# Five of eleven pairs of SwiGLU tiles as seven products of quarters, with weight sums prepared on GpSimd during the input stage

## The chip, the cores and the metric

One core of a Trainium2 chip runs the kernel. The metric is device time in microseconds (us), from one launch of the whole program. Before the change it took 819.53 us, the median of 3 runs (818.77 to 819.92). A measurement is a device time; the profile is one further execution with the hardware profiler on.

## The reference, cut to what matters

One hybrid decoder block in float32, on 512 tokens (T) of width 1024 (D), batch 1, depth 1; the SwiGLU width is 2816.

```python
h = rmsnorm(x, norm1_g)
z = h @ w_in + b_in                              # 1024 -> 6656 columns
z_glu, z_rx, z_rg, z_ga, z_gb = split(z)
u = z_glu[..., :1024] * sigmoid(z_glu[..., 1024:])
y_a = silu(layernorm(causal_conv31(u))) @ conv_w_out + conv_b_out
xb = causal_conv4(z_rx)
y_b = (rg_lru(xb) * gelu(z_rg)) @ lru_w_out
x = x + (sigmoid(z_ga) * y_a + sigmoid(z_gb) * y_b) @ w_mix_out
h = rmsnorm(x, norm2_g)
x = x + (silu(h @ ffn_w1) * (h @ ffn_w3)) @ ffn_w2
return rmsnorm(x, norm_f_g)
```

The change concerns `silu(h @ ffn_w1) * (h @ ffn_w3)` alone; both weights are 1024 x 2816.

## The kernel before

**Numbers.** Each float32 operand is held as two tiles, h (the value cast to the matmul's float32r) and l (the value minus h). A product is three matmuls, h.h, h.l and l.h, which add up in one PSUM bank (`mm3`, L354 to L364; L363 is the matmul). Tokens move: the stationary operand is a 128 x 128 block of weights, the moving one 128 channels by 512 tokens. So a tile of 128 output columns from 1024 inputs is 8 blocks of 3, 24 matmuls of 512 columns.

**Stages.** In order: norm 1; the input stage, which makes all tiles of z in the order that the list `ORDER` gives (62 entries: u, rx, rg, gb, ga are tiles of z, g the small block-diagonal gates of the recurrence, r its scans), with the convolutions on VectorE beside it; lru_w_out (yb), conv_w_out (ya), w_mix_out (mx), norm 2; the SwiGLU stage; the output stage with ffn_w2 (o); and the last norm.

**Weights.** `wchunk` lists all weight chunks in the order of use, and `weights(key)` (L150) hands one out and first emits the list up to four further chunks (AHEAD). `emit_chunk` (L124) takes a raw tile, 128 x 1024 float32, from a pool of 4; loads it by a DMA that the sync engine (SP) issues (L133; L177 for the gates); casts it on ScalarE (ACT, L108) into the h half of one of 5 hl tiles; and subtracts (L104) into the l half. The engine of the subtraction is the argument `lo`: GpSimd (POOL) for w_in and the gates, VectorE (DVE) for all later weights. SP is one queue in program order for all DMAs. A raw tile that has not come free holds SP, and all that is queued behind it. A gate chunk (L168) is put together from small loads. Gates also need rows of neighbouring tiles: `ext_in` (L611 to L623) moves them with small DMAs out of the split tiles of xb, and `gates(j)` (L628 to L643) multiplies them in.

**Seven products, already there.** Two of the matrix products (w_mix_out and ffn_w2) already run by Winograd's form of Strassen's scheme: with both operands cut into quarters, seven products of quarters replace eight. `Quartered` holds the quarters of the weights. Four of the seven weight operands are sums of quarters: t1 = b12 - b11, t2 = b22 - b12 + b11, t3 = b22 - b12, t4 = b21 - t2. `make_sums(k)` makes them for one block row: it loads two raw tiles, runs four 512-column operations on DVE, and stores four results in DRAM (for ffn_w2; 256 KB each), from where they are loaded like weights. `Sevenfold` (from L727) holds the activations' side: `tile` collects the tiles, `pair(k, ua, va)` makes the sums of activations when both tiles of a pair are there, `run` issues the products.

**SwiGLU stage.** The 22 tiles of 128 columns go in pairs k = 0 to 10, tile k and then tile k + 11. A tile is two `mm3` of 512 columns (w1 and w3, banks f1 and f3), then `ffn_out`: a Silu on ACT, and on DVE two products of 256 columns into u or v (L878). With a pair's second tile come `pair` and `outq.make_sums` for ffn_w2. Pair 0 is issued by token halves, 256 columns at a time, because the second half's normalized tokens come later (`turned`, in `turn_half`). Pairs 1 to 10 follow at 512 columns.

**What sets the order.** The program is written for the tile framework, which schedules each engine's instructions by their order of emission and dependences, picks the slots of pools, and adds the semaphores. `issue_after(turned)` keeps what is inside it behind that instruction.

Of the kernel before, what the change touches and what calls it, by code (L numbers as in the profile page):

```python
# [8 lines left out]
F32 = mybir.dt.float32  # L9
F32R = mybir.dt.float32r  # L10
AF = mybir.ActivationFunctionType
ALU = mybir.AluOpType

P = 128
T = 512
# [11 lines left out]
ND = D // P  # L27
NR = DR // P
NF = DF // P
# [8 lines left out]
FEW, MANY = 32, 112  # L38

LAG = 12  # L40


ROWS = [
# [32 lines left out]
def tile_block(ctx, tc, a, out):  # L76
    nc = tc.nc
    pool = lambda name, bufs, **k: ctx.enter_context(tc.tile_pool(name=name, bufs=bufs, **k))
    consts = pool("consts", 1)
    raws = pool("raws", RAW)  # L80
# [4 lines left out]
    def tiles(tag, bufs):  # L85
        p_ = pool(tag, bufs)
        return lambda name, dtype=F32: p_.tile([P, T], dtype, tag=tag, name=name)

    longt, shortt = tiles("long", SLOTS), tiles("short", SHORT)

    def pairt(name, dtype=F32R):

        return longt(f"{name}h", dtype), longt(f"{name}l", dtype)

    def bank(name):
        return psum.tile([P, T], F32, tag="mm", name=name)

    def bank2(name):
        return psum2.tile([P, T], F32, tag="cv", name=name)

    vec, act, pe, pool_e = nc.vector, nc.scalar, nc.tensor, nc.gpsimd

    def sub(eng, o, x, y):
        eng.tensor_tensor(out=o, in0=x, in1=y, op=ALU.subtract)  # L104

    def split_to(h, l, full, eng, copy=act.copy):

        copy(h, full)  # L108
        sub(eng, l, full, h.bitcast(F32))
        return h, l  # L110

    def split(name, full, eng, p_=None, copy=act.copy):
        p_ = p_ or pairt(name)
        return split_to(*p_, full, eng, copy)
# [6 lines left out]
    def wchunk(key, src, kt, cols, where="hl", lo=pool_e, after=None):  # L121
        chunks.append((key, src, kt, cols, where, lo, after))
# [23 lines left out]
    def emit_to(n):  # L146
        while emitted[0] < min(len(chunks), n):
            emit_chunk()

    def weights(key, ahead=AHEAD):  # L150
        i = next(i for i, c in enumerate(chunks) if c[0] == key)
        emit_to(i + 1 + ahead)
        return held.pop(key)
# [36 lines left out]
    ORDER = """u0 u1 rx0 rx1 gb0 rx2 u2 g0 rx3 gb1 g1 u3 rx4 g2 gb2 r0 r1 u4 g3 rx5 rg0 g4 rx6 rg1 u5 r2 r3 g5 rx7  # L190
        gb3 rg2 rx8 g6 rg3 u6 r4 r5 g7 rx9 gb4 rg4 u7 g8 r6 r7 rg5 gb5 g9 rg6 gb6 r8 r9 rg7 gb7 ga0 rg8 ga1 rg9
        ga2 ga3 ga4 ga5 ga6 ga7""".split()
    ORDER = [(t.rstrip("0123456789"), int(t.lstrip("abcdefghijklmnopqrstuvwxyz"))) for t in ORDER]
# [18 lines left out]
    dram = ctx.enter_context(tc.tile_pool(name="dram", bufs=1, space=bass.MemoryType.DRAM))  # L212
# [67 lines left out]
    mixq = Quartered("mx", a["w_mix_out"][0].rearrange("(k p) n -> p k n", p=P), ND // 2, vec, ("t1", "t4"))  # L280
    w1 = a["ffn_w1"][0].rearrange("(k p) n -> p k n", p=P)
    w3 = a["ffn_w3"][0].rearrange("(k p) n -> p k n", p=P)
    ff_order = [j for k in range(NF // 2) for j in (k, k + NF // 2)]
    for j in ff_order:
        wchunk(f"f1_{j}", w1[:, :, j * P : (j + 1) * P], ND, P, lo=vec)
        wchunk(f"f3_{j}", w3[:, :, j * P : (j + 1) * P], ND, P, lo=vec)
    outq = Quartered("o", a["ffn_w2"][0].rearrange("(k p) n -> p k n", p=P), NF // 2, vec)
    x2_kept = [[dram.tile([P, T], F32, tag=f"x2k{t}{h}", name=f"x2k{t}{h}") for h in range(2)] for t in range(NT)]

# [6 lines left out]
    at, col, parts = 0, {}, []  # L296
    for name, n in ROWS:
# [4 lines left out]
        while done < n:  # L302
            m = min(n - done, P - row_at(at + done)[1])
# [50 lines left out]
    def mm3(ps, ws, xs, lo_last=False):  # L354


        n = 3 * len(ws)
        i = 0
        three = [((wh, xh), (wh, xl), (wl, xh)) for (wh, wl), (xh, xl) in zip(ws, xs)]
        if lo_last:  # L360
            three = [q[:2] for q in three] + [q[2:] for q in three]
        for l, r in (q for qs in three for q in qs):
            pe.matmul(ps, l, r, start=i == 0, stop=i == n - 1)  # L363
            i += 1  # L364

    def w_tiles(key, kt, ahead=AHEAD):
        h, l = weights(key, ahead)
        return [(h[:, k, :], l[:, k, :]) for k in range(kt)]
# [41 lines left out]
    def parts_of(pair_tiles, cs=slice(0, T)):  # L410
        return [(h[:, cs], l[:, cs]) for h, l in pair_tiles]
# [9 lines left out]
    HALVES = [slice(0, 256), slice(256, 512)]  # L421
    EARLY = 2
# [42 lines left out]
    ab, e, s, s2, po, c4 = (sm[:, i, :] for i in range(6))  # L465
# [44 lines left out]
    def beside():  # L510
# [18 lines left out]
        def column_mean(name, tot, scale):  # L529

            ps = bank2(f"{name}p")
            for i, v in enumerate(tot):
                pe.matmul(ps, onesr, v, start=i == 0, stop=i == 1)
            act.activation(ps, ps, AF.Copy, scale=scale)
            return ps

        def pause(n):
            for _ in range(n):
                yield
# [6 lines left out]
        tot = split("lnms", tot, vec)  # L546
        yield from pause(LAG)
        mean = column_mean("lnm", tot, 1.0 / DC)
# [10 lines left out]
        tot = split("lnvs", tot, vec)  # L559
        yield from pause(LAG)  # L560
        rs = column_mean("lnv", tot, 1.0 / DC)
# [12 lines left out]
    def run_beside(n):  # L574
        for _ in range(n):
            next(side, None)
# [49 lines left out]
    hs = xb  # L626
# [54 lines left out]
        vec.tensor_tensor(out=ps, in0=hs[j], in1=ps, op=ALU.mult)  # L681
        y.append(split(f"y{j}", ps, vec))

    for kind, j in ORDER:
        if kind == "u":
            glu(j)
        elif kind == "rx":
            rx(j)
            run_beside(4)
        elif kind == "g":  # L690
            gates(j)
        elif kind == "r":
            recur(j)
        elif kind == "rg":
            rg(j)
            run_beside(6)
        elif kind == "gb":
            sig(GB, j, sgb, "sgb")
            run_beside(6)
        else:  # L700
            sig(GA, j, sga, "sga")
            run_beside(8)


    for j in range(8):
        ws = w_tiles(f"lo{j}_0", 5) + w_tiles(f"lo{j}_1", 5)
        ps = bank(f"yb{j}")
# [9 lines left out]
    add = lambda o, x, y: vec.tensor_tensor(out=o, in0=x, in1=y, op=ALU.add)  # L717
    LO, HI = HALVES
# [8 lines left out]
    class Sevenfold:  # L727
# [28 lines left out]
        def product(self, banks, i, x_, w_, start, stop, again=False):  # L756

            (xh, xl), (wh, wl) = x_, w_
            ts = slice(i * P, (i + 1) * P)
            for n, (l_, r_) in enumerate(((xh, wh), (xh, wl), (xl, wh))):  # L760
                pe.matmul(banks[i], l_[:, ts], r_, start=start and n == 0, stop=stop and n == 2, skip_group_check=again)  # L761
# [51 lines left out]
    for n, j in enumerate(mixq.order()):  # L813
        ws = w_tiles(f"co{j}", ND)
        ps = bank(f"ya{j}")
# [12 lines left out]
    h2p = [pairt(f"h2{c}") for c in range(ND)]  # L828
# [42 lines left out]


    o7 = Sevenfold(outq)

    def ffn_out(j, p1, p3):
        s_ = shortt(f"si{j}")
        act.activation(s_, p1, AF.Silu)
        o7.tile(j, lambda cs, dst: vec.tensor_tensor(out=dst, in0=s_[:, cs], in1=p3[:, cs], op=ALU.mult))  # L878
        if j >= NF // 2:
            with tc.issue_after(turned):  # L880
                outq.make_sums(j - NF // 2)

    first_two = ff_order[:EARLY]
    wf = [(w_tiles(f"f1_{j}", ND, 0), w_tiles(f"f3_{j}", ND, 0)) for j in first_two]
    pf = [(bank(f"f1_{j}"), bank(f"f3_{j}")) for j in first_two]
    for hf in range(2):
        if hf:
            turned = turn_half("th", xs, "norm2_g", h2p, 1, [bank2])
# [3 lines left out]
    h2 = parts_of(h2p)  # L892
    with tc.issue_after(turned):
        emit_to(emitted[0] + 3)
    for i, j in enumerate(first_two):
        ffn_out(j, *pf[i])
    for j in ff_order[EARLY:]:
        p1, p3 = bank(f"f1_{j}"), bank(f"f3_{j}")
        mm3(p1, w_tiles(f"f1_{j}", ND), h2)
        mm3(p3, w_tiles(f"f3_{j}", ND), h2)  # L900
        ffn_out(j, p1, p3)


    x2 = [[longt(f"x2b{t}{h}") for h in range(2)] for t in range(NT)]
# [93 lines left out]
```

## Time and profile before

| | us |
|---|---|
| median of 3 runs | 819.53 |
| profiled execution, device time | 819.27 |
| its span in the profile | 817.5 |
| PE busy | 805.6 (99%) |
| DVE / ACT / POOL busy | 607.6 / 420.0 / 149.7 |
| input stage (28 to 312) | 284.0 |
| SwiGLU, pair 0 (461 to 487.5) | 26.5 |
| SwiGLU, pairs 1 to 10 (487.5 to 705) | 217.5 |
| output stage (705 to 817.5) | 112.5 |

PE is the matmul engine and PEld its weight loads, which run beside it; DVE is VectorE, ACT ScalarE, POOL GpSimd, and SPq the queue of SP that issues DMAs. Lines (L363) are the kernel's. POOL works only until the end of the input stage: in the page's 40 slices it is idle from the sixteenth on.

```profile
POOL 3564456535534530000000000000000000000000
```

Each digit is the busy share of 20.4 us in tenths. The granted TensorE clock of the execution was 0.997.

### The profile page before, as it was taken

Reading aid. Unit: us, or ns where it says so; the run is one execution under the profiler, and the core shown is the slowest. Engines: PE = TensorE matmul, PEld = TensorE weight load, DVE = VectorE, ACT = ScalarE, POOL = GpSimd, SP = SyncE. Lnnn points to the kernel's source line nnn. Section 1 sums busy time; section 2 is a strip of 40 time slices with the busy share of each in tenths; the row PEclk is TensorE's granted clock in tenths of the full one; section 3 lists DMA queues with packets and bytes.
Section 4 is the critical chain, followed back from the end, with each engine's and each line's share of the span. In section 5 each row is a group of like instructions: output and inputs, shape, how many; then the busy total and the mean of one; then the engine's idle time right before and its main releaser. Section 6 shows DMA issues by size and latency. Waiting matters only on the chain.

```text
span 817.5 us, 10585 instructions
## 1 busy us (share of the span) xinstructions
PE 805.6 (99%) x3750; PEld 673.7 (82%) x3750; DVE 607.6 (74%) x954; ACT 420.0 (51%) x587; POOL 149.7 (18%) x84
## 2 busy tenths in 40 slices
PE   8999999999999999999999999999999999999996
PEld 7988888888888888888888998888888888888885
DVE  4699999999989976876968866455555444688556
ACT  7546688778678565743336543222222222476443
POOL 3564456535534530000000000000000000000000
PEclk9999999999999999999999999999999999999998
DMA  6634433444323412369538448656665666876552
GB/s 207 168 97 117 122 92 102 111 108 112 101 85 110 132 49 67 114 196 292 169 126 248 148 134 267 190 178 204 193 181 187 198 194 205 263 265 205 171 165 103
DMA packets 158343, 130.31 MB, mean 159 GB/s; under 512 B 11367, under 2 KB 128531, under 8 KB 158291
## 3 DMA queue, kind: packets, MB, share of 16 engines
q1 hardware_dynamic: 158291, 129.65, 52.1%
q8 instruction: 29, 0.48, 0.2%
q14 instruction: 23, 0.19, 0.1%
HBM read 108.78 MB, written 17.83 MB: 155 GB/s over the span
## 4 chain that ended last, share of the span: by engine, by line
PE 96%; DMA 1%; SPq 1%; DVE 0%; POOL 0%; ACT 0%; issue 0%
PE z L363 34%; PE f L363 29%; PE or L761 13%; PE yb L363 7%; PE ya L363 5%; PE mxr L761 5%; PE g L643 3%; DMA raw_in<-in_w_in_dram 1%; SPq L319 1%; PE th L403 0%; SPq L312 0%; POOL hl_in L104 0%; DVE of L921 0%; ACT hl_in L108 0%; SPq L133 0%
## 5 line engine op out<-in xcount | busy, mean ns | idle before, releaser
L522 DVE SCALAR_TENSOR_TENSOR cv<-u,par,cv 128x511 f32<-128x511 f32 (+17 forms) x240 | 162.6, 728 | 1.4 <-ACT cv L519 1.2
L104 POOL TENSOR_TENSOR hl_in<-raw_in,hl_in 128x1024 fp32r<-128x1024 f32 x52 | 125.6, 2419 | 136.6 <-ACT hl_in L108 131.8
L108 ACT CAST hl_f<-raw_f 128x1024 fp32r<-128x1024 f32 x44 | 46.2, 1053 | 143.5 <-PE f L363 81.1
L104 DVE TENSOR_TENSOR hl_f<-raw_f,hl_f 128x1024 fp32r<-128x1024 f32 x44 | 53.8, 1222 | 37.4 <-ACT hl_f L108 37.3
L108 ACT CAST hl_in<-raw_in 128x1024 fp32r<-128x1024 f32 x52 | 54.2, 1043 | 11.3 <-PE z L363 7.1
L878 DVE TENSOR_TENSOR ou<-si,f 128x256 f32<-128x256 f32 x22 | 9.3, 422 | 62.2 <-PE f L363 61.6
L108 ACT CAST hl_ob<-raw_ob 128x1024 fp32r<-128x1024 f32 (+1 forms) x23 | 23.4, 1016 | 42.4 <-PE or L761 19.3
L363 PE MATMUL z<-h10h,hl_in 128*128 128x512 f32 (+1 forms) x112 | 42.3, 379 | 1.2 <-DVE h10l L407 0.9
L104 DVE TENSOR_TENSOR hl_ob<-raw_ob,hl_ob 128x1024 fp32r<-128x1024 f32 (+1 forms) x23 | 27.0, 1176 | 19.7 <-ACT hl_ob L108 19.5
L363 PE MATMUL z<-h14h,hl_in 128*128 128x512 f32 (+1 forms) x112 | 41.7, 374 | 0.0
L363 PE MATMUL z<-h13h,hl_in 128*128 128x512 f32 (+1 forms) x112 | 41.7, 374 | 0.0
L363 PE MATMUL z<-h15h,hl_in 128*128 128x512 f32 (+1 forms) x112 | 41.7, 374 | 0.0
L363 PE MATMUL z<-h16h,hl_in 128*128 128x512 f32 (+1 forms) x112 | 41.7, 374 | 0.0
L363 PE MATMUL z<-h11h,hl_in 128*128 128x512 f32 (+1 forms) x112 | 41.7, 374 | 0.0
L363 PE MATMUL z<-h17h,hl_in 128*128 128x512 f32 (+1 forms) x112 | 41.7, 374 | 0.0
L363 PE MATMUL z<-h12h,hl_in 128*128 128x512 f32 (+1 forms) x112 | 41.7, 374 | 0.0
L363 PE MATMUL f<-h22h,hl_f 128*128 128x512 f32 (+1 forms) x96 | 35.4, 371 | 0.0
L363 PE MATMUL f<-h23h,hl_f 128*128 128x512 f32 (+1 forms) x96 | 35.4, 372 | 0.0
L363 PE MATMUL f<-h25h,hl_f 128*128 128x512 f32 (+1 forms) x96 | 35.4, 372 | 0.0
L363 PE MATMUL f<-h24h,hl_f 128*128 128x512 f32 (+1 forms) x96 | 35.4, 371 | 0.0
L363 PE MATMUL f<-h26h,hl_f 128*128 128x512 f32 (+1 forms) x96 | 35.4, 371 | 0.0
L363 PE MATMUL f<-h20h,hl_f 128*128 128x512 f32 (+1 forms) x96 | 35.0, 373 | 0.3 <-ACT h20h L406 0.3
(812 smaller groups left out, 2258.0 us busy)
## 6 DMA issues: line engine op xcount, KB each, us to landing
raw_in<-in_w_in_dram SPq DMA_DIRECT2D x52, 512.0 KB
raw_f<-in_ffn_w_dram SPq DMA_DIRECT2D x44, 512.0 KB
ows<-in_ffn_w_dram SPq DMA_DIRECT2D x22, 512.0 KB
ot<-ows SPq DMA_DIRECT2D x44, 256.0 KB
raw_ob<-in_ffn_w_dram SPq DMA_DIRECT2D x33, 256.0 KB
raw_ot<-ot SPq DMA_DIRECT2D x33, 256.0 KB
raw_lo<-in_lru_w_out_dram SPq DMA_DIRECT2D x16, 320.0 KB
x<-in_x_dram SPq DMA_DIRECT2D x16, 256.0 KB
```

Of the source, the lines that this page charges most:

```text
L104: eng.tensor_tensor(out=o, in0=x, in1=y, op=ALU.subtract)
L108: copy(h, full)
L319: nc.sync.dma_start(xt[t][h], x_nat[:, t, h * T : (h + 1) * T])
L363: pe.matmul(ps, l, r, start=i == 0, stop=i == n - 1)
L522: vec.scalar_tensor_tensor(out=acc[c][:, s:], in0=u[c][:, : T - s], scalar=dw(c, s), in1=acc[c][:, s:], op0=ALU.mult, op1=ALU.add)
L643: pe.matmul(ps, l, r, start=k == 0, stop=k == len(mms) - 1)
L761: pe.matmul(banks[i], l_[:, ts], r_, start=start and n == 0, stop=stop and n == 2, skip_group_check=again)
L878: o7.tile(j, lambda cs, dst: vec.tensor_tensor(out=dst, in0=s_[:, cs], in1=p3[:, cs], op=ALU.mult))
```

## The change

Pairs 2 to 6 (`SEVEN`) of the SwiGLU stage are computed by the seven products too. The activations h2 are cut into quarters: channels 0 to 511 and 512 to 1023 by tokens 0 to 255 and 256 to 511. The weights' quarters are channels by tile k or tile k + 11. One pair is then seven products of 4 channel blocks, each with 3 matmuls for w1 and 3 for w3, so 24 matmuls of 256 moving columns: w1's result stands in the left half of a bank and w3's in the right. Five banks (r1, r2, r3, r5, r7) collect them; r1 is used three times in a pair, for b11, then t2, then t4, which goes on top of t2. ACT copies and DVE adds join them into the four quarters of u and v (`out_of` is Silu on ACT, then a product of 256 columns on DVE).

The weight chunks of such a pair are seven (b11, b21, b22, t1 to t4; 1024 columns each, two loads for a b, one for a t) where there were four. The t sums are made in the input stage by `make_f_sums`, on GpSimd, in 20 pieces: one ahead of every third entry of `ORDER` from entry 4 on. A piece takes one raw tile, four loads of 128 KB, four operations of 256 columns and four stores of 128 KB. The activations' sums are made once by `f_inputs`, behind `turned`: eight additions of 512 columns on GpSimd (h + l), sixteen operations of 256 columns and eight splits on ACT and DVE. The output weights' `make_sums` no longer comes with each pair: two follow pair 1, one each pair 3 and pair 5, two each pair 7, 8 and 9; pair 0 has none, pair 10 what is left.

The diff, without its added blank lines:

```diff
@@ -38,6 +38,10 @@
 FEW, MANY = 32, 112
 LAG = 12
+SEVEN = (2, 3, 4, 5, 6)
+SUMS_AT, SUMS_STEP = 4, 3
 ROWS = [
@@ -280,10 +284,50 @@
     mixq = Quartered("mx", a["w_mix_out"][0].rearrange("(k p) n -> p k n", p=P), ND // 2, vec, ("t1", "t4"))
     w1 = a["ffn_w1"][0].rearrange("(k p) n -> p k n", p=P)
     w3 = a["ffn_w3"][0].rearrange("(k p) n -> p k n", p=P)
-    ff_order = [j for k in range(NF // 2) for j in (k, k + NF // 2)]
-    for j in ff_order:
-        wchunk(f"f1_{j}", w1[:, :, j * P : (j + 1) * P], ND, P, lo=vec)
-        wchunk(f"f3_{j}", w3[:, :, j * P : (j + 1) * P], ND, P, lo=vec)
+    KF = NF // 2
+    f_sums = {(n, k): dram.tile([P, 1024], F32, tag=f"f{n}_{k}", name=f"f{n}_{k}") for k in SEVEN for n in ("t1", "t2", "t3", "t4")}
+    def f_quarter(n, k, w_, c0, c1):
+        c, j = 4 * (int(n[1]) - 1), k + KF * (int(n[2]) - 1)
+        return w_[:, c + c0 : c + c1, j * P : (j + 1) * P]
+    def f_chunk(n, k):
+        def load(raw_t):
+            if n[0] == "t":
+                nc.sync.dma_start(raw_t, f_sums[n, k][:, :])
+            else:
+                for i, w_ in enumerate((w1, w3)):
+                    nc.sync.dma_start(raw_t[:, i * T : (i + 1) * T].rearrange("p (k n) -> p k n", k=4), f_quarter(n, k, w_, 0, 4))
+        wchunk(f"f{n}_{k}", load, 8, P, lo=vec)
+    def make_f_sums(k, i, c):
+        names = ("b11", "b12", "b21", "b22")
+        raw = raws.tile([P, 1024], F32, tag="raw", name=f"fws{k}_{i}_{c}")
+        q11, q12, q21, q22 = q = [raw[:, 256 * n : 256 * n + 256] for n in range(4)]
+        for n, v in zip(names, q):
+            nc.sync.dma_start(v.rearrange("p (k n) -> p k n", k=2), f_quarter(n, k, (w1, w3)[i], c, c + 2))
+        sub(pool_e, q22, q22, q12)
+        sub(pool_e, q12, q12, q11)
+        pool_e.tensor_tensor(out=q11, in0=q22, in1=q11, op=ALU.add)
+        sub(pool_e, q21, q21, q11)
+        at = T * i + P * c
+        for n, v in (("t1", q12), ("t2", q11), ("t3", q22), ("t4", q21)):
+            nc.sync.dma_start(f_sums[n, k][:, at : at + 256], v)
+    for k in range(KF):
+        if k in SEVEN:
+            for n in ("b11", "b21", "b22", "t1", "t2", "t3", "t4"):
+                f_chunk(n, k)
+        else:
+            for j in (k, k + KF):
+                wchunk(f"f1_{j}", w1[:, :, j * P : (j + 1) * P], ND, P, lo=vec)
+                wchunk(f"f3_{j}", w3[:, :, j * P : (j + 1) * P], ND, P, lo=vec)
     outq = Quartered("o", a["ffn_w2"][0].rearrange("(k p) n -> p k n", p=P), NF // 2, vec)
     x2_kept = [[dram.tile([P, T], F32, tag=f"x2k{t}{h}", name=f"x2k{t}{h}") for h in range(2)] for t in range(NT)]
@@ -681,7 +725,10 @@
         vec.tensor_tensor(out=ps, in0=hs[j], in1=ps, op=ALU.mult)
         y.append(split(f"y{j}", ps, vec))
-    for kind, j in ORDER:
+    pieces_left = [(k, i, c) for k in SEVEN for i in range(2) for c in (0, 2)]
+    for n, (kind, j) in enumerate(ORDER):
+        if n >= SUMS_AT and (n - SUMS_AT) % SUMS_STEP == 0 and pieces_left:
+            make_f_sums(*pieces_left.pop(0))
         if kind == "u":
             glu(j)
         elif kind == "rx":
@@ -871,16 +918,22 @@
     o7 = Sevenfold(outq)
+    sums_of = iter(range(KF))
+    def out_sums(n):
+        with tc.issue_after(turned):
+            for _ in range(n):
+                k = next(sums_of, None)
+                if k is not None:
+                    outq.make_sums(k)
     def ffn_out(j, p1, p3):
         s_ = shortt(f"si{j}")
         act.activation(s_, p1, AF.Silu)
         o7.tile(j, lambda cs, dst: vec.tensor_tensor(out=dst, in0=s_[:, cs], in1=p3[:, cs], op=ALU.mult))
-        if j >= NF // 2:
-            with tc.issue_after(turned):
-                outq.make_sums(j - NF // 2)
-    first_two = ff_order[:EARLY]
+    first_two = [0, KF]
     wf = [(w_tiles(f"f1_{j}", ND, 0), w_tiles(f"f3_{j}", ND, 0)) for j in first_two]
     pf = [(bank(f"f1_{j}"), bank(f"f3_{j}")) for j in first_two]
     for hf in range(2):
@@ -894,11 +947,87 @@
         emit_to(emitted[0] + 3)
     for i, j in enumerate(first_two):
         ffn_out(j, *pf[i])
-    for j in ff_order[EARLY:]:
-        p1, p3 = bank(f"f1_{j}"), bank(f"f3_{j}")
-        mm3(p1, w_tiles(f"f1_{j}", ND), h2)
-        mm3(p3, w_tiles(f"f3_{j}", ND), h2)
-        ffn_out(j, p1, p3)
+    f_in = {n: [] for n in ("a11", "a12", "a22", "s1", "s2", "s3", "s4")}
+    def f_inputs():
+        for k in range(4):
+            a1, a2 = [longt(f"hf{c}") for c in (k, k + 4)]
+            for v, c in ((a1, k), (a2, k + 4)):
+                pool_e.tensor_tensor(out=v, in0=h2p[c][0].bitcast(F32), in1=h2p[c][1].bitcast(F32), op=ALU.add)
+            g = [longt(f"hs{k}_{i}") for i in range(2)]
+            s1, s2, s3, s4 = (v[:, cs] for v in g for cs in HALVES)
+            add(s1, a1[:, HI], a2[:, HI])
+            sub(vec, s2, s1, a1[:, LO])
+            sub(vec, s3, a1[:, LO], a1[:, HI])
+            sub(vec, s4, a2[:, LO], s2)
+            s12, s34 = [split(f"hs{k}_{i}", v, vec) for i, v in enumerate(g)]
+            for n, p_, cs in (
+                ("a11", h2p[k], LO), ("a12", h2p[k + 4], LO), ("a22", h2p[k + 4], HI),
+                ("s1", s12, LO), ("s2", s12, HI), ("s3", s34, LO), ("s4", s34, HI),
+            ):
+                f_in[n].append(tuple(v[:, cs] for v in p_))
+    with tc.issue_after(turned):
+        f_inputs()
+    def ffn_seven(k):
+        u_, v_ = longt(f"ou{k}"), longt(f"ov{k}")
+        def product(ps, x_, w_, again=False):
+            h, l = weights(f"f{w_}_{k}")
+            for i in range(2):
+                for c, (xh, xl) in enumerate(f_in[x_]):
+                    for m, (lw, rx_) in enumerate(((h, xh), (h, xl), (l, xh))):
+                        pe.matmul(
+                            ps[:, HALVES[i]], lw[:, 4 * i + c, :], rx_, start=not (again or i or c or m),
+                            stop=bool(i and c == 3 and m == 2), skip_group_check=True,
+                        )
+        def out_of(c, dst):
+            act.activation(c[:, LO], c[:, LO], AF.Silu)
+            vec.tensor_tensor(out=dst, in0=c[:, LO], in1=c[:, HI], op=ALU.mult)
+        r1, r2, r3, r5, r7 = bank(f"fr1_{k}"), bank2(f"fr2_{k}"), bank(f"fr3_{k}"), bank2(f"fr5_{k}"), bank(f"fr7_{k}")
+        product(r1, "a11", "b11")
+        c11 = shortt(f"c11_{k}")
+        act.copy(c11, r1)
+        product(r2, "a12", "b21")
+        add(c11, r2, c11)
+        out_of(c11, u_[:, LO])
+        product(r3, "s4", "b22")
+        product(r5, "s1", "t1")
+        product(r1, "s2", "t2", True)
+        q = shortt(f"q_{k}")
+        act.copy(q, r1)
+        add(q, r5, q)
+        c12 = shortt(f"c12_{k}")
+        add(c12, r3, q)
+        out_of(c12, u_[:, HI])
+        product(r7, "s3", "t3")
+        c21 = shortt(f"c21_{k}")
+        act.copy(c21, r7)
+        add(q, r7, q)
+        out_of(q, v_[:, HI])
+        product(r1, "a22", "t4", True)
+        add(c21, r1, c21)
+        out_of(c21, v_[:, LO])
+        o7.uv.append((u_, v_))
+        o7.pair(k, u_, v_)
+    for k in range(1, KF):
+        if k in SEVEN:
+            ffn_seven(k)
+            out_sums(k % 2)
+            continue
+        for j in (k, k + KF):
+            p1, p3 = bank(f"f1_{j}"), bank(f"f3_{j}")
+            mm3(p1, w_tiles(f"f1_{j}", ND), h2)
+            mm3(p3, w_tiles(f"f3_{j}", ND), h2)
+            ffn_out(j, p1, p3)
+        out_sums(2 if k < KF - 1 else KF)
     x2 = [[longt(f"x2b{t}{h}") for h in range(2)] for t in range(NT)]
```

## Prediction

> **What bounds the kernel now.** I read the page's first part and its chain, then the windows by stage, then the chain in order of time.
>
> ```profile
> span 817.5 us, 10585 instructions
> PE 805.6 (99%) x3750; PEld 673.7 (82%) x3750; DVE 607.6 (74%) x954; ACT 420.0 (51%) x587; POOL 149.7 (18%) x84
> PE 96%; DMA 1%; SPq 1%; DVE 0%; POOL 0%; ACT 0%; issue 0%
> ```
>
> PE is busy for 99% of the span and makes up 96% of the chain that ended last. So the time is PE's time, and every other engine matters only where it makes PE wait.
>
> ```profile
> 28.00:312.00 284.00, 284.00 (x1297) 236.82 (x1296) 267.38 (x413) 193.65 (x239) 137.81 (x74) 1.00 0.38 104
> 461.00:487.50 26.50, 26.16 (x213) 25.45 (x212) 17.77 (x33) 14.07 (x27) 0.00 (x0) 1.00 0.34 106
> 487.50:705.00 217.50, 217.50 (x962) 180.16 (x961) 115.47 (x182) 60.69 (x81) 0.00 (x0) 1.00 0.65 203
> 705.00:817.50 112.50, 105.03 (x463) 86.36 (x461) 77.33 (x107) 58.13 (x85) 0.00 (x0) 0.98 0.59 194
> ```
>
> The columns are the length of the stage, the busy time of PE, PEld, DVE, ACT and POOL, the granted clock, the DMA share and GB/s. The rows are the input stage, the first SwiGLU pair (0), the other ten pairs, and the output stage. In the stages that the change touches PE has no gap: 284.00 of 284.00 and 217.50 of 217.50. In the SwiGLU pairs DVE is half idle. In the input stage DVE is 94% busy and POOL not quite half.
>
> ```profile
> 246.68 65.30 PE z L363 x288
> 311.98 0.46 PE lnmp L533 x2
> 461.61 11.51 PE f L363 x96
> 478.61 226.43 PE f L363 x1033
> 705.04 102.97 PE or L761 x453
> ```
>
> These are start, length and count in the chain. The first row is all of 512 moving columns: 65.30/288 = 226.7 ns a matmul. The third is the first token half of pair 0, all of 256 columns: 11.51/96 = 119.9 ns. So half the columns cost 53% of the time, since each matmul pays about 13 ns beside its columns.
>
> **What the products save.** A pair by the old way is 96 matmuls of 512 columns, 96 x 226.7 = 21.77 us. By seven products it is 7 x 24 = 168 matmuls of 256, 168 x 119.9 = 20.14 us. The arithmetic falls by an eighth, but the 13 ns is now paid 168 times, and 1.62 us of the pair is left. Five pairs: **-8.1 us**. The rest of PE's order is unchanged.
>
> [...]
>
> **Work beside PE in pairs 2 to 6.** These rows are of the SwiGLU stage: DVE's, then ACT's.
>
> ```profile
> L104 DVE TENSOR_TENSOR hl_f<-raw_f,hl_f 128x1024 fp32r<-128x1024 f32 x41 | 50.1, 1221 | 35.6 <-ACT hl_f L108 35.6
> L104 DVE TENSOR_TENSOR ows<-ows,ows 128x512 f32<-128x512 f32 x22 | 15.1, 688 | 1.0 <-DMA ows<-in_ffn_w_dram 0.7
> L878 DVE TENSOR_TENSOR ou<-si,f 128x256 f32<-128x256 f32 x21 | 8.9, 422 | 59.4 <-PE f L363 58.7 <-ACT si L877 0.7
> L717 DVE TENSOR_TENSOR x<-mxr,x 128x512 f32<-128x512 f32 x6 | 3.8, 679 | 0.0
> L108 ACT CAST hl_f<-raw_f 128x1024 fp32r<-128x1024 f32 x41 | 43.1, 1053 | 139.8 <-PE f L363 81.1 <-issue 52.5 <-DMA raw_f<-in_ffn_w_dram 6.2
> L108 ACT CAST ous2h<-ou 128x512 fp32r<-128x512 f32 x1 | 0.6, 617 | 0.0
> ```
>
> Per new pair DVE has seven weight subtractions (8.5 us), five adds with a bank (5 x 0.68 = 3.4), four products of 256 columns (1.7), the pair's own sums (0.69 + 5 x 0.42 = 2.8), and in pairs 3 and 5 the output weights' sums (4 x 0.69 = 2.8): 16.4 or 19.2 us in 20.14. ACT has 7 x 1.053 of casts, three copies at 0.62, four Silu of 256 columns and the casts of the pair, some 12 us. Both fit. A weight chunk is now needed every 24 x 0.1199 = 2.88 us rather than every 5.44. Five hl buffers let a chunk's cast begin four products ahead, 11.5 us; cast and subtraction take 2.3 us of it, so about 9 us is left for queues. I take 0 for pairs 3 to 6.
>
> One wait is new: bank r1 is used three times in a pair, and the copy that frees it after t2 (on ACT) has only the t3 product's 2.88 us. Ahead of it on ACT stands the cast of the next pair's b21, so a load that comes late holds the copy, then PE, then everything behind the copy on ACT.
>
> Pair 2 is the tight one. Between the end of pair 0's second half, 478.6 us, and the subtraction of its t2 weights DVE has nine weight subtractions (11.0), the input sums (16 x 0.42 + 8 x 0.69 = 12.2), two sets of output-weight sums (8 x 0.69 = 5.5), pairs 0 and 1 (8 x 0.42 and 2 x 2.8 = 9.0): 37.7 us. Pair 2 begins at 705.0 - 9 x 21.77 = 509.1, and its t2 product 4 x 2.88 later, at 520.6: 42.0 us for 37.7 of work, much of which waits for casts that PE's own pace sets. The weight sums hold all four raw buffers there, too, and t4 and the next b11 and b21 load only behind their stores. I take **+2 us**; bounds 0 and 6.4, the latter if GpSimd's eight adds of h2 stop DVE for their whole length: 8 x 1.34 = 10.7, less the 4.3 of room.
>
> ```profile
> L104 POOL TENSOR_TENSOR hl_in<-raw_in,hl_in 128x1024 fp32r<-128x1024 f32 x52 | 125.6, 2419 | 136.6 <-ACT hl_in L108 131.8 <-PE g L643 2.9 <-DMA raw_gate<-in_lru_wa_dram 1.4
> L104 POOL TENSOR_TENSOR hl_gate<-raw_gate,hl_gate 128x512 fp32r<-128x512 f32 x10 | 13.4, 1340 | 14.1 <-ACT hl_gate L108 9.8 <-DMA raw_gate<-in_lru_wx_dram 4.2
> 297.18 1.90 DVE L542 TENSOR_TENSOR lnmt<-u,u 128x512 f32<-128x512 f32 x1
> 296.13 2.40 POOL L104 TENSOR_TENSOR hl_in<-raw_in,hl_in 128x1024 fp32r<-128x1024 f32 x1 [2.72 <-ACT hl_in L108]
> ```
>
> That they can stop each other is in the last two rows. A DVE add of 512 columns with both operands in SBUF takes 1.90 us rather than 0.69, and ends 0.55 us after the POOL subtraction that ran (298.53). [...]
>
> **The input stage.** Twenty pieces are added, each four 128 KB loads, four POOL operations of 256 columns and four stores, one in three places of the list of 62. PE gives a piece 284/62 x 3 = 13.7 us. From the two rows, 256 columns take POOL about 1.34 - 1.08/2 = 0.80 us, an estimate, so 3.2 us a piece. Its present work is 137.81/20 = 6.9 us. If POOL also stands idle while a piece lands, that adds 2 to 5 us: 512 KB at the 203 GB/s of the pairs' row is 2.6 us, and the chain's slowest such wait, at the start, is below.
>
> ```profile
> 17.72 5.11 DMA raw_in<-in_w_in_dram
> 150.25 2.55 SPq L177 DMA_DIRECT2D raw_gate<-in_lru_wx_dram  x5
> 153.54 0.55 SPq L623 DMA_DIRECT2D ext<-xb6h  x1
> 154.77 1.21 SPq L623 DMA_DIRECT2D ext<-xb6h  x2
> 159.94 0.40 PE L643 MATMUL g<-ext,hl_gate 96*128 96x512 f32 x1
> SPq L133 <- POOL hl_in L104: 130.7, 37, 9.5
> ```
>
> POOL's loop is then 3.2 + 6.9 + 2.6 = 12.7 us of 13.7, 15.2 at worst. SP adds 8 issues of 0.51 us, 4.1 us a piece. SP is in order, and a piece's stores wait on it for POOL; behind them wait the next w_in loads, the gates' loads and the ext copies. For w_in chunks there is cover: a chunk is cast when the one five before it ends, four chunks or 21.8 us ahead, less 1.05 and 2.42, some 18 us (14 with a gate chunk among them). The ext copies have little. Those for gate 5 are issued from 153.54 to 155.98 and PE reads them at 159.94. In the changed order SP has, ahead of them, the stores of piece (3, 1, 2) and two loads of piece (4, 0, 0), which wait until those stores have landed. Following SP and POOL from piece to piece with these durations, I get the copies 1 to 7 us later, against some 2.5 us to spare once their landing is counted. I take **+2.5 us**, bounds 0 and 5. A PE that has waited there gives every later chunk the same room, so I count it once. The row of lnmp (311.98) needs sums that DVE has ready at about 306.9; 5.1 us covers seven adds that wait 0.8 us each but for 0.5. I take 0.
>
> **Sum.** The profiled execution took 819.27 us, 817.5 of them the span. 819.27 - 8.1 + 2.0 + 2.5 = 815.7; the median of the runs, 819.53, is 0.26 above that execution, so **815.9 us**. With no stall it is 811.4; with both upper bounds 819.5 - 8.1 + 6.4 + 5.0 = 822.8.
>
> **Rivals.** (1) *The loop of SP and POOL is too slow for the input stage.* The mechanism is the in-order stores; the place is pieces 8 to 16, where gates, ext copies and pieces meet. It decides when a piece's loop passes 13.7 us by more than the cover: over twenty pieces 14 us, so above 14.4 us a loop. At 14.9 it costs 20 x 1.2 - 14 = 10 us, and 819.5 - 8.1 + 2 + 10 = 823; at the worst of 15.2 us, 829. For it: SP already waits 130.7 us for POOL to free raw buffers, and a piece holds one of only four for a load, four sums and a store. Against: 12.7 us by the middle values, and PE's queue runs 14 us behind POOL. Chance 0.24, **slower**.
>
> (2) *Pairs 2 to 6 do not run at PE's pace.* [...] 5 x 1.6 = 8 us is the whole gain: 819.5. For it: pair 2's margin is 4.3 us before any lock. Against: 9 us of cover in the others. Chance 0.15, no change.
>
> [...] Chance 0.04. [...]
>
> **How the numbers follow.** The forecast, 811.4 to 817.8, has 0.57; with (3), faster has 0.61, no change 0.15, slower 0.24. A measurement of this kernel tells about 0.2% (1.6 us) from no change. The range runs from 811, no stall, to 823, both upper bounds and the start of rival (1); some 0.12 lies above and 0.05 below.
>
> **What would show it.** Right: matmuls into the banks fr1 to fr7 with 119.9 ns from start to start, about 100.7 us in the chain for pairs 2 to 6 against 108.8; a gap before gate 5's ext matmul of some 2 us and one in pair 2; nothing else on PE. Rival (1) would show as PE waits for POOL hl_in in several places and a window 28 to 312 that is over 290 long. Rival (2) would show as waits of PE for ACT's copies of r1 or for hl_ft in each pair, and POOL and DVE rows above 1.34 and 1.22 us around 480 us. The forecast is wrong if the input stage grows by over 6 us, or the five pairs take over 107.

## The result, and the profile after

The changed kernel takes **847.29 us** (median of 4 runs, 846.01 to 849.39) against 819.34 before: a ratio of 1.0344, 95% interval 1.0321 to 1.0366. It is 28 us slower; forecast were 3.6 us less. The page of its profile, span and busy times:

```profile
span 847.6 us, 11862 instructions
PE 810.1 (96%) x4110; PEld 691.9 (82%) x4110; DVE 653.3 (77%) x1018; ACT 449.5 (53%) x634; POOL 222.8 (26%) x172
```

PE is busy longer than before (805.6), although its work shrank. The starts of the stages' first matmuls in the two traces tell where (yb is the first stage behind the input stage, f the SwiGLU stage, or the output stage):

| | first yb | first f | first or | end of span | SwiGLU | output |
|---|---|---|---|---|---|---|
| before | 323.2 | 461.4 | 704.9 | 817.5 | 243.5 | 112.6 |
| after | 359.0 | 497.3 | 734.8 | 847.6 | 237.5 | 112.8 |

The input stage ends 35.8 us late, SwiGLU is 6.0 us shorter, the rest is as it was. The waits of PE in the changed kernel (us in total, times, longest):

```profile
PE g L687 <- DMA ext<-xb6h: 7.1, 1, 7.1
PE z L407 <- DVE xb L644: 3.7, 1, 3.7
PE z L407 <- POOL hl_in L108: 3.6, 2, 3.3
PE z L407 <- DVE xb L711: 3.1, 1, 3.1
PE z L407 <- DVE u L630: 2.9, 1, 2.9
PE g L687 <- DVE y3l L108: 1.8, 1, 1.8
PE fr L984 <- ACT q L1004: 1.8, 1, 1.8
```

All but the last lie in the input stage, but for 0.3 of the 3.6 us, which are ahead of it. PE's eight gaps there are 3.7 (at 115 us), 7.1 (174), 1.8 and 0.6 (220), 3.1 (226), 2.9 (266), 1.5 (288) and 3.3 (314): 24.1 us. One of them ends with GpSimd and one with a copy for gate 5; six, 13.6 us in all, end with VectorE, which before was busy 94% of this stage. What VectorE and GpSimd waited for, before and after (fws is the tile of a piece):

```profile
DVE hl_gate L182 <- POOL hl_gate L104: 4.5, 5, 1.2
```

```profile
DVE hl_gate L186 <- POOL hl_gate L108: 15.9, 5, 6.9
DVE xb L644 <- ACT xb L642: 10.0, 4, 4.2
POOL fws L108 <- DMA fws<-in_ffn_w_dram: 73.5, 17, 8.6
```

VectorE copies part of each gate chunk (L186) and comes to it while GpSimd has not yet cut it, because GpSimd, in order, stands before a piece that has not landed: 73.5 us in 17 waits, 4.3 us a time. One such case, rows of GpSimd, then VectorE:

```profile
127.67 1.55 POOL L108 TENSOR_TENSOR fws<-fws 128x256 f32<-128x256 f32 x2 [4.68 <-DMA fws<-in_ffn_w_dram]
130.82 2.21 POOL L108 TENSOR_TENSOR hl_gate<-raw_gate,hl_gate 128x512 fp32r<-128x512 f32 x2
```

```profile
132.15 0.28 DVE L186 CAST hl_gate<-raw_gate 32x256 fp32r<-32x256 f32 x1 [3.65 <-POOL hl_gate L108]
```

A second way goes by SP and ScalarE. SP's stores wait for the sums, the gate's loads stand behind them, ScalarE's cast of the gate waits for those loads, and behind the cast stands the step that VectorE's convolution of xb needs. Two of the four waits for ScalarE, 6.8 us of the 10.0 (before, such waits were 0.5 in all), came so; one, of 2.7 us, only follows from PE's own gap at 174. Rows of SP, ScalarE and VectorE:

```profile
226.85 4.52 SPq L321 DMA_DIRECT2D ft<-fws  x4
234.00 2.53 SPq L181 DMA_DIRECT2D raw_gate<-in_lru_wx_dram  x5
```

```profile
238.09 0.62 ACT L112 CAST hl_gate<-raw_gate 128x512 fp32r<-128x512 f32 x1 [3.96 <-DMA raw_gate<-in_lru_wx_dram]
```

```profile
239.43 0.75 DVE L644 SCALAR_TENSOR_TENSOR xb<-z,par,xb 128x511 f32<-128x511 f32 x1 [4.22 <-ACT xb L642]
```

That the gaps go through VectorE is read from the trace; no run takes its waits away alone. The other part of the loss is the clock. PE after the first gap (start, length), and PE by windows (length, busy of PE, PEld, DVE, ACT, POOL, then granted clock, DMA share, GB/s):

```profile
115.08 0.76 PE L407 MATMUL z<-h10h,hl_in 128*128 128x512 f32 x1 [3.73 <-DVE xb L644]
115.64 0.63 PE L407 MATMUL z<-h10l,hl_in 128*128 128x512 f32 x1
116.07 0.63 PE L407 MATMUL z<-h10h,hl_in 128*128 128x512 f32 x1
...
120.31 0.40 PE L407 MATMUL z<-h14h,hl_in 128*128 128x512 f32 x1
120.55 0.40 PE L407 MATMUL z<-h14l,hl_in 128*128 128x512 f32 x1
```

```profile
174.00:178.00 4.00, 4.00 (x10) 3.17 (x10) 2.80 (x5) 2.46 (x3) 0.68 (x1) 0.50 0.35 91
160.00:220.00 60.00, 51.12 (x216) 41.50 (x214) 48.28 (x71) 38.27 (x49) 38.48 (x30) 0.94 0.53 143
```

From 115.64 to 116.07 the spacing is 0.43 us, from 120.31 to 120.55 it is 0.24: for 3 to 5 us behind each of the five long gaps it stays 0.43 us: half the clock (0.50 granted in the row of 174). Summed over the matmuls behind all gaps, spacing less 226.7 ns, that is 10.3 us. Gaps and slow clock make 34.4 of the 35.8 us. The five gaps of 2.9 us and more have 1.7 to 2.5 us behind them, those of 1.5 and 1.8 us 0.1 each.

### The profile page after: what moved, and what is told of

It is laid out like the page before. It is cut to its first block, busy times and chain, and to the rows that moved or that the text cites. A ratio compares the mean times of both kernels' runs of the same rounds, so it can differ in the third digit from the quotient of the medians.

```text
span 847.6 us, 11862 instructions
## 1 busy us (share of the span) xinstructions
PE 810.1 (96%) x4110; PEld 691.9 (82%) x4110; DVE 653.3 (77%) x1018; ACT 449.5 (53%) x634; POOL 222.8 (26%) x172
## 5 line engine op out<-in xcount | busy, mean ns | idle before, releaser
L566 DVE SCALAR_TENSOR_TENSOR cv<-u,par,cv 128x511 f32<-128x511 f32 (+17 forms) x240 | 162.6, 729 | 1.6 <-ACT cv L563 1.3
L108 POOL TENSOR_TENSOR hl_in<-raw_in,hl_in 128x1024 fp32r<-128x1024 f32 x52 | 125.3, 2417 | 36.7 <-ACT hl_in L112 35.8
L112 ACT CAST hl_in<-raw_in 128x1024 fp32r<-128x1024 f32 x52 | 54.2, 1042 | 35.9 <-DMA raw_in<-in_w_in_dram 32.5
L108 POOL TENSOR_TENSOR fws<-fws 128x256 f32<-128x256 f32 x60 | 45.5, 758 | 86.2 <-DMA fws<-in_ffn_w_dram 73.5
L407 PE MATMUL z<-h10h,hl_in 128*128 128x512 f32 (+1 forms) x112 | 44.6, 400 | 14.9 <-DVE xb L644 3.7
L112 ACT CAST hl_f<-raw_f 128x1024 fp32r<-128x1024 f32 x24 | 25.1, 1051 | 36.5 <-DMA raw_f<-in_ffn_w_dram 17.1
L407 PE MATMUL z<-h11h,hl_in 128*128 128x512 f32 (+1 forms) x112 | 43.6, 391 | 0.0
L108 DVE TENSOR_TENSOR hl_f<-raw_f,hl_f 128x1024 fp32r<-128x1024 f32 x24 | 31.6, 1319 | 12.2 <-ACT hl_f L112 12.2
L407 PEld LDWEIGHTS z<-h10h,hl_in 128*128 128x128 f32 x112 | 22.0, 196 | 21.3 <-POOL hl_in L108 4.2
L644 DVE SCALAR_TENSOR_TENSOR xb<-z,par,xb 128x511 f32<-128x511 f32 (+2 forms) x30 | 22.3, 742 | 10.0 <-ACT xb L642 10.0
L984 PE MATMUL fr<-hs_0h,hl_ft 128*128 128x256 f32 x160 | 29.6, 283 | 0.0
L108 DVE TENSOR_TENSOR hl_ft<-raw_ft,hl_ft 128x1024 fp32r<-128x1024 f32 x20 | 24.3, 1219 | 6.2 <-ACT hl_ft L112 6.2
L108 DVE TENSOR_TENSOR hl_ot<-raw_ot,hl_ot 128x1024 fp32r<-128x1024 f32 (+1 forms) x17 | 20.1, 1189 | 11.4 <-ACT hl_ot L112 11.0
```

Of the source, the lines that this page charges most:

```text
L566: vec.scalar_tensor_tensor(out=acc[c][:, s:], in0=u[c][:, : T - s], scalar=dw(c, s), in1=acc[c][:, s:], op0=ALU.mult, op1=ALU.add)
L644: vec.scalar_tensor_tensor(out=o[:, s:], in0=ps[:, : T - s], scalar=lw(s), in1=o[:, s:], op0=ALU.mult, op1=ALU.add)
L984: pe.matmul(ps[:, HALVES[i]], lw[:, 4 * i + c, :], rx_, start=not (again or i or c or m), stop=bool(i and c == 3 and m == 2), skip_group_c ...
```

## The experiments

The theories: **A**, a piece holds one of four raw tiles; **B**, the sums are too much work for GpSimd; **D**, SP issues too many DMAs; **E**, GpSimd and SP, both in order, wait for each other (GpSimd for a piece's landing, SP's stores for GpSimd), and work and waits of the round add up; **F**, SP's wait for the sums alone. "No pieces" is the floor. Where no interval is given, the time is of one run; the runs of one kernel lay 1 to 5 us apart, so a difference of 2 us between two such times says little.

**Without pieces.** `pieces_left = []`, the t chunks load rows of ffn_w2.

> The pieces are left out of the input stage, and the t chunks load rows of ffn_w2 of the same size in place of the sums, so the SwiGLU stage does the same work on other numbers. Theory A (the pieces hold raw tiles and stand in SP's queue, so that the input stage is bound by landing, sum and store one after the other) and theory B (GpSimd has too much work with the sums) agree here: yb begins at 323 us as before, not at 359, and only the gain of the five pairs is left, 819.3 - 6 = 813.3 us, 812.5 to 814.5. If the input stage stays longer than 285 us, the cause is neither.

813.66 us (811.95 to 814.97), ratio 0.9933 [0.9914, 0.9951]. First yb 322.5, SwiGLU 238.3. So the new pairs alone are a gain of 5.5 us, and the pieces cost 33.6.

**One part of a piece left out.**

```diff
-        sub(pool_e, q22, q22, q12)      # and the other three: no_ops
-            nc.sync.dma_start(f_sums[n, k][:, at : at + 256], v)      # no_stores
```

> The four GpSimd operations of a piece are left out; a piece is loaded and stored as it is. All 160 added DMA issues stay. Theory B (GpSimd's work): 20 x 3.1 us go from GpSimd, and the time is that without pieces, 813 to 816 us. Theory A (tiles and queue): a piece still holds its tile from the issue of its loads to the end of its stores, some 8 us rather than 11, and SP still waits in it, so a good part of the 36 us stays: 822 to 838 us. Theory D (SP's issues, 8 x 0.5 us a piece): 840 to 848 us.

815.64 us: as B has it, and not A or D. The 160 issues, the same raw tiles and all the added traffic cost 2 us by themselves; the DMA engines are busy for 0.64 of the window from 28 to 312 us, against 0.53 to 0.62 in the change's windows there, so a full DMA is not the cause either. But the landing waits of GpSimd go with its operations, so E is not excluded.

> Loads and GpSimd's sums of the pieces stay, the stores are left out (80 of the 160 issues), and the t chunks load rows of ffn_w2. Theory B: GpSimd's work is the same, 843 to 848 us. Theory A: SP does not stop for the sums any more, except where it finds no free raw tile, and the tile comes free some 2 to 4 us earlier: 815 to 830 us. Theory D: half of the issues, about half of the loss, 825 to 832 us.

826.58 us: within A's range and D's; B has to fall or share, since GpSimd's work is whole.

**A tile of its own.** `raw = [longt(...) for n in range(2)]`.

> A piece takes two tiles of the long pool (69 of 128 x 512) in place of one of the four raw tiles; everything else is the change. Theory A, if the tile is what counts: SP finds a raw tile for w_in earlier, and the loss falls to 0 to 15 us, 813 to 828 us. Theory A, if the stores' wait in SP's queue is what counts: 835 to 847 us. Theory B and theory D: 845 to 848 us, as the work and the issues are the same.

830.31 us, between the ranges: half the loss goes. The raw tile matters, but not alone: in no_ops, where nothing waits for GpSimd, pieces in raw tiles cost 2 us.

**Work and waits apart.** tiny:

```diff
-        sub(pool_e, q22, q22, q12)
+        sub(pool_e, q22[:, :2], q22[:, :2], q12[:, :2])
```

> The four operations of a piece work on 2 of their 256 columns, so GpSimd still waits for the landing and SP's stores for GpSimd, and most of the work, about 2.6 of 3.1 us a piece, is gone. Theory E (work and waits add up): the measured round of 15.5 us falls to 12.9, under PE's 13.7, and little is lost, 814 to 820 us, while GpSimd's waits for fws stay at 50 to 90 us. Theory B: 813 to 816 us with GpSimd's waits of no account. If the waits alone decide: 830 us or more.

830.55 us. Nearly without work, half the loss stays, with these waits (of GpSimd); B falls, and E's 814 to 820 too: waits alone do this.

```profile
POOL fws L108 <- DMA fws<-in_ffn_w_dram: 66.4, 17, 7.4
```

work_only has the four operations on two resident tiles:

> The four operations of a piece work on two resident tiles and not on the piece; it is loaded and stored as it is. GpSimd has all the work and no landing to wait for. Theory E: the round is 15.5 - 4.3 = 11.2 us, 813 to 817 us. Theory B: the work is there, so the loss is, 835 to 848 us.

867.39 us, which tells nothing: with nothing to wait for, the scheduler moved the operations to the start, where they held up the first w_in chunks.

```profile
PE z L412 <- POOL hl_in L108: 35.7, 3, 16.6
```

So each piece's four were pinned (`tc.issue_after` puts them behind the last subtraction before them):

> The four operations of a piece work on two resident tiles, as in work_only, but each piece's four are queued behind the w_in subtraction emitted last before them, so that they cannot all be moved to the start. Loads and stores of the pieces stay and don't touch GpSimd. Theory E (the round of GpSimd is work plus landing waits plus what SP's stores hold up): 20 x 3.1 us of work alone fit in GpSimd's 136 idle us, 814 to 819 us. Theory B (the work itself): 828 to 848 us.

816.92 us. All the work, all DMAs, no landing that GpSimd waits for and no store that waits for GpSimd: 3.3 us over the floor. **B is out**, and so is any blocking of VectorE by GpSimd's sums as the main cause, as all the sums are here. Work alone costs 3.3 us, waits alone 16.9 (tiny), both 33.6, 13 us more than the two added up. That fits one round in which work and waits follow each other, as E has it, though E's figure for tiny was 11 us too low. So the loss needs the dependence between the pieces and GpSimd; how much of it is GpSimd's wait and how much SP's, this pair does not tell.

**The waits taken away.** Tiles of their own, and sums one place (three entries) behind the loads:

```diff
-            make_f_sums(*pieces_left.pop(0))
+            landed.append(make_f_sums(*pieces_left.pop(0)))
+            if len(landed) > 1:
+                landed.pop(0)()      # sums and stores of the piece before
```

> As own (tiles of the long pool), and a piece's sums and stores are emitted one place later, three entries of the list behind its loads. The same work and the same DMAs. Theory E (GpSimd works in order and waits for each piece's landing, 73.5 us in 17 waits, and the w_in subtractions behind it wait too; with work and waits its round of a piece is longer than PE's 13.7 us): the landing waits go, the round is 3.2 + 6.9 us and some casts, 813 to 817 us, no PE gap over 1 us in the input stage. Theory B (the sums' work, 3.1 us a piece): as own, 828 to 832 us. If SP's wait for the stores in its queue holds the w_in loads: 820 to 830 us.

830.68 us (ratio 1.0151 [1.0126, 1.0177]): as own, because the scheduler put the sums right behind the loads again (55.8 us of waits for fws left). The same in a raw tile:

> The sums and stores one place later, but the piece in a raw tile as in the change, so that one or two of the four raw tiles are always taken. Theory E, if landing waits alone count: 813 to 818 us. Theory A (raw tiles): w_in has two or three tiles, SP waits for them longer than before, 825 to 850 us.

838.3 us, in A's range: 8 us more than in a tile of its own, 9 less than the change, so here the same move did help. Now own_late with the sums pinned, own_behind:

```diff
             if len(landed) > 1:
-                landed.pop(0)()
+                with tc.issue_after(pool_sub[0]):      # the last subtraction on GpSimd
+                    landed.pop(0)()
```

> As own_late, but the sums of a piece are queued on GpSimd behind the w_in subtraction emitted last before them, three entries behind the loads; so far the scheduler had put them right behind the loads again (55.8 us of GpSimd's landing waits were left in own_late). Theory E: GpSimd's waits for fws fall under 15 us, and the time to 814 to 821 us, with the gap at gate 5 at most. If SP's queue (loads and stores in order, ext copies behind them) is the bound by itself: the waits of GpSimd go, and the time stays at 826 to 832 us.

824.35 us, between E's range and that of SP's queue. The waits fell from 55.8 to 19.9 us, and the time by 6.3 us. Of the 33.6 us, 23 are gone now, but 17 of them went with the tile of its own.

```profile
POOL fws L110 <- DMA fws<-in_ffn_w_dram: 19.9, 5, 9.1
```

**Fewer pieces, other places.** three:

```diff
-SEVEN = (2, 3, 4, 5, 6)
-SUMS_AT, SUMS_STEP = 4, 3
+SEVEN = (2, 3, 4)
+SUMS_AT, SUMS_STEP = 4, 5
```

> Three new pairs (2 to 4) with 12 pieces, one ahead of every fifth entry; the rest as in the change. PE takes 22.9 us for five entries. Theory E: GpSimd's round is 11.5 us of w_in and gate work, 3.2 of sums, 4.3 of landing and 1.8 of casts, 20.8 us, so PE does not wait but at gate copies: 819.3 - 3 x 2.0 / 2 + 0 to 6, 816 to 822 us. Theory A (a piece's tile and its place in SP's queue cost the same 1.8 us each wherever it stands): 12 x 1.8 - 4 = 17 us more, 830 to 836 us.

825.54 us: both missed. First yb is 5.7 us late though PE has 22 us for a piece: so waits cost even where the round is not full, it seems through VectorE, which waited 14.6 us for gate chunks (4.5 before). SwiGLU gains nothing either (244.6 us): pair 2 waits 3.0 us. moved_own takes the pieces out of the loop over `ORDER`:

```diff
         if j in (2, 4, 6):
             mixq.make_sums(j // 2 - 1)
+        make_f_sums(*pieces_left.pop(0))      # after each yb; after each ya one or two
```

> The pieces are taken out of the input stage and made in the stages yb (one a tile) and ya (one or two a tile), where GpSimd has nothing else to do and the weights' subtractions are VectorE's; the pieces take tiles of the long pool. Theory E: the landing waits on GpSimd hold up nobody, and only SP's order is left; the input stage is back at yb = 323 us, and yb and ya grow by 0 to 6 us, 813 to 820 us. If SP's waits for the stores are the bound by themselves: yb and ya lose 10 us and more, 823 to 835 us.

900.88 us, far outside both ranges. The input stage is back (first yb at 323.0), but GpSimd has nothing else to do in yb and ya, and there it is far worse. PE waits for the casts of w_mix_out's weights; SP's stores of the pieces, ahead of the weights' loads, wait 36 us for the sums:

```profile
PE mxr L807 <- ACT hl_mxb L112: 48.5, 5, 19.2
```

```profile
SPq L321 <- POOL fws L108: 36.0, 37, 4.7
```

**The rest of the loss.** coal has one store for four (`f_sums` is then one tile of 128 x 4 x 1024 for each pair):

```diff
-        for n, v in (("t1", q12), ("t2", q11), ("t3", q22), ("t4", q21)):
-            nc.sync.dma_start(f_sums[n, k][:, at : at + 256], v)
+        nc.sync.dma_start(f_sums[k][:, :, at : at + 256], raw.rearrange("p (q n) -> p q n", q=4))
```

> The four results of a piece are kept side by side in DRAM, so that one store of 512 KB takes the place of four of 128 KB: 100 added DMA issues rather than 160; the rest as in the change. Theory D (the number of issues and of DMAs in flight): the loss falls to about five eighths, 833 to 837 us. Theory F (SP stands still from a piece's loads until GpSimd has done its last sum, however many stores follow): as the change, 843 to 849 us.

850.25 us, a little above F's range: fewer issues gain nothing, so D is out as the main cause, as it was in no_ops. One store starts only after the last sum, and the gap at gate 5 is 11.4 us. piped has the stores one place later still, pinned on SP:

```diff
+            if len(summed) > 1:
+                with tc.issue_after(raw_load[0]):      # the last w_in load on SP
+                    summed.pop(0)()
```

> As own_behind, with a piece's stores one place later still, queued on SP behind the w_in load emitted last before them; loads, sums and stores of a piece are then three places of the list. Theory F: SP's 31 us of waits for the sums go, 815 to 820 us. If what is left of the loss in own_behind (10.7 us over the kernel without pieces) lies in the number of DMAs that SP issues: 822 to 826 us.

822.0 us, at D's edge, but it is no test of F: SP's waits for the sums are still 28.1 us (30.9 in own_behind). own_behind_pool removes them:

```diff
-                nc.sync.dma_start(f_sums[n, k][:, at : at + 256], v)
+                pool_e.dma_start(f_sums[n, k][:, at : at + 256], v)
```

> As own_behind, with the stores issued by GpSimd behind its own sums and not by SP: 80 issues and all waits for the sums are gone from SP. What an issue costs GpSimd no run here shows. Theory F: up to about 1 us each fits in its idle time, 815 to 820 us; if an issue takes 2 us and more, GpSimd's round passes PE's 13.7 us, 825 us and more.

824.87 us, though SP hardly waits for the sums any more (2.1 us in the trace): F's 815 to 820 is missed. It is no clean test of F, since GpSimd now pays for the issues itself (us busy, mean ns of one, idle ahead), and the gap at gate 5 is 6.8 us:

```profile
L327 POOL DMA_DIRECT2D ft<-fws x80 | 44.3, 555 | 0.0
```

> Both cuts together: two tiles for the pieces in a pool of their own (the long pool has 65 in place of 69), sums queued behind the w_in subtraction emitted last before them, one place behind the loads, and one store for the four results. Theories E and F: neither queue waits for the other, and 60 issues are gone: 814 to 818 us, below the 819 of before. Theory D gives 818 to 822 us. If four tiles fewer in the long pool cost the later stages something: over 822 us.

822.08 us (1.0033 [1.0021, 1.0046]). The input stage ends 5.5 us late and the output stage is 4.8 us longer, perhaps for the four tiles; that was not tried alone. The queues did not come free of each other: SP still waits 40.8 us for the sums. Last, piped with two stores of two results each, and the same with other places:

```diff
-SUMS_AT, SUMS_STEP = 4, 3
+SUMS_AT = (4, 7, 9, 12, 14, 17, 19, 30, 33, 35, 38, 40, 43, 46, 48, 51, 53, 56, 58, 61)      # piped2_g5
```

> As piped (loads, sums and stores of a piece in three successive places, tiles of the long pool, all 69 of them), with the four results kept so that two stores take the place of four: 120 added issues rather than 160. Theories E and F (in-order waits of SP and GpSimd): as piped or a little better, 819 to 822 us. Theory D (number of issues): 8.4 us of loss over the kernel without pieces fall by a quarter, 818 to 820 us.

> As piped2, with the twenty pieces at other places of the list: none at entries 21 to 28, where the small copies for gate 5 are issued (the largest PE gap of the change, 7.1 us, and still 0.9 us in piped), the others closer together. If the copies for gate 5 are held up by pieces ahead of them in SP's queue: no gap there, 1 to 3 us less than piped2, 816 to 819 us. If the pieces that stand closer together elsewhere cost as much: the same as piped2 or up to 4 us more.

820.87 us (1.0022 [1.0012, 1.0032]), in the range of E and F, and 823.00 (1.0053 [1.0041, 1.0065]). At gate 5 PE has no gap any more in piped2_g5, but new ones of 1.7, 1.0, 0.7 and 2.3 us at 235 to 264, where the pieces stand closer. No version with the pieces beats the kernel before. In the order tried, the tile of its own took 17 us of the loss, the later sums 6, later and fewer stores 3 or 4; another order could share this out otherwise. 7 us over the floor stay, and which of VectorE's, SP's and GpSimd's small waits they are made of stays open.

## Why the prediction was wrong

- **What the products save: right.** Pairs 2 to 6 take 102.8 us, 544.9 to 647.7, against 5 x 21.77 = 108.9: -6.0, where -8.1 + 2.0 was forecast. Less the wait below that is 120 ns for each of 840 matmuls. Rival (3), with 0.04, counted on these running closer together than pair 0's 119.9 ns, and rival (2), with 0.15, on 1.6 us lost in each pair; no run shows the first, and of these five pairs PE waits in pair 2 alone, 1.79 us.
- **Pair 2: right, place and mechanism.** PE waits 1.79 us, before the t4 product, for ACT's copy of r1 (q), which stands behind the cast of an fb chunk that landed late. That the size came out too (1.79 for 2) is partly luck: it was weighed from VectorE's room, and VectorE is not what PE waits for. The rows are PE's, then ACT's:

```profile
564.07 0.38 PE L984 MATMUL fr<-h24h,hl_ft 128*128 128x256 f32 x1 [1.79 <-ACT q L1004]
```

```profile
562.49 1.04 ACT L112 CAST hl_fb<-raw_fb 128x1024 fp32r<-128x1024 f32 x1 [0.81 <-DMA raw_fb<-in_ffn_w_dram]
563.44 0.58 ACT L1004 COPY q<-fr 128x512 f32<-128x512 f32 x1
```

- **GpSimd's adds stop VectorE: right, and covered.** 512 columns take GpSimd 1.29 us where it starts ahead of VectorE's subtractions and 2.27 beside them; these take 2.0 (4.02 for two) and not 1.22. Rows of GpSimd, then VectorE:

```profile
513.53 1.29 POOL L958 TENSOR_TENSOR hf<-h24h,h24l 128x512 f32<-128x512 f32 x1 [2.02 <-DVE h24l L451]
...
516.03 2.27 POOL L958 TENSOR_TENSOR hf<-h25h,h25l 128x512 f32<-128x512 f32 x1
```

```profile
515.36 4.02 DVE L108 TENSOR_TENSOR hl_f<-raw_f,hl_f 128x1024 fp32r<-128x1024 f32 x2
```

- **The input stage, the step that failed:** "I take +2.5 us, bounds 0 and 5", and its reason "a PE that has waited there gives every later chunk the same room, so I count it once". The place was right (gate 5's ext copies, behind pieces in SP's queue, the longest gap at 7.1 us), the count was not. PE waited eight times: 24.1 us of gaps and 10.3 of slow clock stand where +2.5 was put. GpSimd's round was put at 12.7 us, 15.2 at worst. The rows are the pieces' loads on SP (ns shortest, median, longest; first and last start) and their sums on GpSimd:

```profile
L314 SPq DMA_DIRECT2D fws<-in_ffn_w_dram x80: 368/468/1162, 38.0 to 334.0; - x80
```

```profile
L108 POOL TENSOR_TENSOR fws<-fws 128x256 f32<-128x256 f32 x60 | 45.5, 758 | 86.2 <-DMA fws<-in_ffn_w_dram 73.5 <-DVE cv L566 10.3
```

  From the first load of all to the first of the last piece (1.4 us ahead of 334.0) it is 294.6 us for 19 rounds, 15.5 each, PE's own waits included. The sums were sized well (0.80 forecast, 0.76 measured); the landing wait was not, 2.6 for 4.3, though its bound of 5 held, and the casts of w_in that came late because SP had issued their loads late (ScalarE waited 32.5 us for them) were left out.
- **PE's time for a piece** was 13.5 us and not 13.7. The list has 64 entries, not 62, and they run on past 312 to the first yb at 323.2, so that two slips nearly cancel, by luck. The first matmuls of gb0 (entry 4) and ga5 (entry 61) start at 50.2 and 306.4: 256.2 us for 19 pieces.
- **Rival (1) is nearest to what came**, with a chance of 0.24 and a price of 823 to 829: the two in-order queues hold each other up, and the input stage grows. Its sign came only in part. It named PE waits for hl_in in several places; there is one (3.3 us), and six are for VectorE. Its sum can't be checked with the 15.5 us, since PE's own pace from gb0 to ga5 fell to 15.4 us a piece (50.3 to 342.2), gaps and slow clock included. The slow clock behind the gaps, 10.3 us, was in no case.
- **VectorE's want of room was seen and not priced.** "Every other engine matters only where it makes PE wait" passed over the 94%: 16.6 us of room in 284, and waits of VectorE that grew by 11.4 us for GpSimd (L186) and by 9.5 for ScalarE (L644).

## What to carry to other kernels

In this kernel the work that was added to an idle engine cost what that engine then waited for, not its busy time: 61 us of sums were nearly free (816.9), and the landing waits in front of them, with the raw tiles and the stores that wait along, were not. Follow each new wait to all who queue behind it, and first to the engine with the least room (here VectorE with 6%); then count what stands behind a PE gap (here gaps of 2.9 to 3.3 us cost 4.6 to 5.0 us with the slow clock behind them). And where a scheduler orders the program, moving a line need not move the instruction as meant; look at the order that results (own_late, work_only).

## What the runs showed of the hardware

- The clock after a gap (the changed kernel): behind gaps of 2.9 to 7.1 us the matmuls of 512 columns stood 0.43 us apart for 3 to 5 us rather than 0.23 (granted clock 0.50 from 174 to 178 us), 1.7 to 2.5 us more for each gap; behind gaps of 1.5 and 1.8 us it was 0.1 us more.
- A DMA issue of 128 KB on GpSimd took 555 ns (own_behind_pool, mean of 80); on SP such stores took 344 ns (the changed kernel, median of 80).
- The convolution's steps on VectorE (one operand in PSUM) were not slower with more of GpSimd's work beside them: in the changed kernel (L566) they took 729 ns on average, the longest of 240 took 756, with 222.8 us of GpSimd's work in the program; before (L522), 728 and 755 with 149.7 us.
